# The front part of an encoder block, written as one list of operations

## The chip, the core and the metric

The kernel runs on one core of a Trainium2 chip. The metric is device time in microseconds (us) of one execution. The engines are TensorE (PE, with its weight load PEld), VectorE (DVE), ScalarE (ACT), GpSimd (POOL) and SyncE (SP), whose queue here issues all DMAs. Each engine works through its own instructions in the order in which the program has them, and waits where an operand or a buffer is not ready.

## The reference

One layer of a bidirectional encoder on 1024 tokens (a grid of 16 rows by 64 columns), with float32 inputs and output:

```python
D_MODEL, SEQ, N_HEADS, HEAD_DIM, CONV_WIDTH, D_FF = 1024, 1024, 8, 64, 512, 4096
...
u = rms_norm(x, norm1_g)
proj = u @ w_in
q, k, v, cb, cc, ch, ga, gb = split(proj)   # widths 512 x 6, 1024 x 2
q = rms_norm(q.reshape(B, S, N_HEADS, HEAD_DIM), q_norm_g)
k = rms_norm(k.reshape(B, S, N_HEADS, HEAD_DIM), k_norm_g)
y_a = neighbourhood_attention(q, k, v, rpb) @ w_attn_branch
y_b = short_gated_conv(cb, cc, ch, conv_w) @ w_conv_branch
merged = sigmoid(ga) * y_a + sigmoid(gb) * y_b
x = x + merged @ w_o
h = rms_norm(x, norm2_g) @ w_mlp_in
x = x + square(relu(h)) @ w_mlp_out

```

`rms_norm` divides by the root of the mean square plus 1e-6 and multiplies by a gain. The neighbourhood attention has 8 heads of 64, a window of 8 rows by 16 columns and a learned position bias. The convolution is depthwise with three taps.

## The kernel before

Every matrix product is made of float16 pairs: an operand is scaled by a power of two, rounded to a float16 "hi", and what is left is a float16 "lo". A product is three passes, hi x hi, hi x lo and lo x hi (`PASSES`), added in one PSUM bank. The scale of a weight follows from its largest entry or from its sum of squares, which a small matmul with a matrix of ones adds up over the 128 partitions (`all_sum`).

Tokens come in 8 blocks of 128. The first stage, up to the fourth Q unit, is the one the change rewrites. In it:

- A block of x is loaded (`load_x`), squared and summed on ACT, its reciprocal root `y` is made by small steps on DVE with a root on ACT (`rstd`), then `u` hi is a scaled copy on ACT (L453) and `u` lo the remainder on DVE (L455). `u` is turned into `UT`, with the model dimension on the partitions: blocks 0 to 2 by PE transposes (`ln_trans`, eight for hi and eight for lo), blocks 3 to 7 by a DMA transpose (`ln_turn`, L470).
- V's weights come in two halves (`cV[0]`, `cV[1]`) of two 512 KB pieces each. The hi parts are made on ACT (L313), the lo parts of the first piece on DVE (L300) and of the second on POOL (L310, L298).
- `v_unit` multiplies one block by one half of V's weights (24 matmuls of 256 columns; blocks 0 to 2) or by both (24 of 512; blocks 3 to 7).
- `sforms` makes sums and differences of quarters of the normalized x on POOL, splits them on ACT and DVE and stores them to DRAM (L522); the gate products of a later stage read them.
- Then come 8 Q units and 8 K units, each 24 matmuls of 512 columns (5.18 us from start to start). Each is followed by a chain `qk_vec`: copy and square on ACT (L610, L611), a reduction per head (L614) and `rstd` on DVE, a product (L621), hi on ACT (L628), lo on DVE (L630), and a DMA transpose of the result into `QD` or `KD` (`finish_qk`, L641). The tiles `q16` that hold hi and lo have two buffers. `QD` takes the place of x in SBUF.

Behind it stand the convolution, attention, the gates, the output projection and the MLP, all of them with PE busy nearly throughout.

What sets the order is how the Python code is run: `unit` emits a group of matmuls, and behind it a number of steps of the generators in `fg` (`step`) and of the weight preparation in `bg` (`tick`). There is no scheduler behind it; an instruction stands in its engine's queue where the code emitted it. Weight pieces go through five buffers (`rawp`), so a piece is loaded when the buffer five pieces back is free.

Of the kernel before, what the change touches and what calls it, by code (L numbers as in the profile page):

```python
# [70 lines left out]
def encoder_block(ctx: ExitStack, tc: tile.TileContext, x, weights, cols, gqk, rel, masks, out):  # L71
# [375 lines left out]
    def norm(xin, sq, u, y):  # L447

        ss = tmp()
        A.activation(sq, xin, AF.Square, accum_out=sc[:, ss])  # L450
# [2 lines left out]
        A.activation(u[:, 0], xin, AF.Copy, scale=sc[:, y])  # L453
        yield
        V.scalar_tensor_tensor(u[:, 1], xin, sc[:, y], u[:, 0], op0=OP.mult, op1=OP.subtract)  # L455

    def ln_trans(u16, b, dst):
        for s in range(2):
            pt = bank16("o")
            for k in range(8):  # L460
                T.transpose(pt[:, k * 128:(k + 1) * 128], u16[:, s, k * 128:(k + 1) * 128], ident)
            o = dst[:, s, :, b * 128:(b + 1) * 128]
            i = pt.rearrange("p (k t) -> p k t", k=8)
            if s == 0:
                A.activation(o, i, AF.Copy)
# [32 lines left out]
    SFORM = (6, 8, 10, 12)

    def sforms():  # L500

        for n, start in enumerate(SFORM):
            yield from apart(start, 0)
            assert turned[0] >= n + 5
            z = []
            for b in (n, n + 4):
                A.activation(xt[:, b], xt[:, b], AF.Copy, scale=sc[:, at(ys, b)])
# [1369 lines left out]
```

## Time and profile before

| | |
|---|---|
| time, median of 3 runs | 1233.58 us (1231.42 to 1234.42) |
| the profiled execution | 1232.41 us, its span 1230.6 us |
| PE busy | 1197.8 us, 97% |
| DVE, ACT, POOL busy | 943.2 (77%), 765.9 (62%), 432.5 us (35%) |
| mean granted clock of PE | 0.994 |
| PE busy in the first 93.7 us | 73.63 us |

A row of the page's time line gives the start (us from the span's start), the length (us), the engine, the line of the kernel, the operation, output and inputs, and, in brackets, how long the engine was idle before it and what ended that wait. "xN" means that N such instructions are taken together. A row of a stretch gives length and busy time by engine with the number of instructions, then the granted clock (1.00 is full), the share of DMA engines busy and GB/s.

### The profile page before, as it was taken

Reading aid. Unit: us, or ns where it says so; the run is one execution under the profiler, and the core shown is the slowest. Engines: PE = TensorE matmul, PEld = TensorE weight load, DVE = VectorE, ACT = ScalarE, POOL = GpSimd, SP = SyncE. Lnnn points to the kernel's source line nnn. Section 1 sums busy time; section 2 is a strip of 40 time slices with the busy share of each in tenths; the row PEclk is TensorE's granted clock in tenths of the full one; section 3 lists DMA queues with packets and bytes.
Section 4 is the critical chain, followed back from the end, with each engine's and each line's share of the span. In section 5 each row is a group of like instructions: output and inputs, shape, how many; then the busy total and the mean of one; then the engine's idle time right before and its main releaser. Section 6 shows DMA issues by size and latency. Waiting matters only on the chain.

```text
span 1230.6 us, 16688 instructions
## 1 busy us (share of the span) xinstructions
PE 1197.8 (97%) x6102; PEld 575.8 (47%) x6102; DVE 943.2 (77%) x1747; ACT 765.9 (62%) x1185; POOL 432.5 (35%) x289
## 2 busy tenths in 40 slices
PE   4989999999999999999999999999999999999998
PEld 3534445555444444444468444444444444444444
DVE  6668778898658686887878555455447899999997
ACT  6777667778645455436768687687775763646430
POOL 2340003231411111101004455665658463464562
PEclk9999999999999999999999999999999999999999
DMA  6457455567551121125197454355374924435202
GB/s 259 105 201 173 105 117 120 127 138 143 112 141 60 45 69 44 61 80 227 32 166 186 149 188 160 131 179 178 131 265 162 366 104 162 171 115 220 104 35 103
DMA packets 170867, 173.34 MB, mean 141 GB/s; under 512 B 131488, under 2 KB 132000, under 8 KB 166688
## 3 DMA queue, kind: packets, MB, share of 16 engines
q1 hardware_dynamic: 170784, 172.27, 47.0%
q8 instruction: 48, 0.79, 0.3%
q14 instruction: 35, 0.29, 0.1%
HBM read 102.51 MB, written 37.75 MB: 114 GB/s over the span
## 4 chain that ended last, share of the span: by engine, by line
PE 40%; DVE 7%; ACT 2%; issue 2%; DMA 1%; DVEq 0%; ACTq 0%
PE ps_d L207 16%; PE ps_s L207 13%; PE ps_o L207 10%; DVE ops L1710 1%; DVE w L1090 1%; DVE form L1281 1%; DVE v L1329 1%; DMA u2T<-v 1%; DMA u2x<-v 1%; DVE ops L1703 0%; DVE x L1464 0%; ACT ops L1701 0%; ACT as L1559 0%; DVE x L1808 0%; DVE as L1603 0%
## 5 line engine op out<-in xcount | busy, mean ns | idle before, releaser
L207 PEld LDWEIGHTS <-ops 128*128 128x128 f16 x1356 | 132.9, 98 | 161.0 <-issue 4.8
L207 PEld LDWEIGHTS <-w 128*128 128x128 f16 x1368 | 133.1, 98 | 143.9 <-issue 5.0
L927 PE MATMUL ps_d<-uT,w_ws 128*128 128x512 f16 x576 | 135.7, 379 | 2.0 <-DVE cv L66 2.0
L207 PE MATMUL ps_s<-ops 128*128 128x512 f16 (+1 forms) x528 | 118.4, 374 | 0.0
L207 PE MATMUL ps_d<-ops 128*128 128x512 f16 x504 | 115.6, 379 | 0.0
L207 PE MATMUL ps_d<-u2T,w 128*128 128x512 f16 (+1 forms) x504 | 110.1, 371 | 0.0
L1701 ACT ACTIVATE ops<-hf,sc 128x2048 f16<-128x2048 f32 x26 | 52.0, 1999 | 93.2 <-PE ps_d L207 51.4
L1077 POOL TENSOR_TENSOR tsum<-raw 128x512 f32<-128x512 f32 x28 | 46.5, 1676 | 148.8 <-ACT raw L959 148.8
L207 PEld LDWEIGHTS <-uT 128*128 128x128 f16 x648 | 64.6, 100 | 70.3 <-issue 6.6
L1281 POOL TENSOR_TENSOR as<-as 128x512 f32<-128x512 f32 x56 | 76.7, 1370 | 41.4 <-ACT as L1561 38.1
L207 PEld LDWEIGHTS <-w_s 128*128 128x128 f16 x588 | 56.9, 98 | 69.3 <-issue 0.9
L927 PEld LDWEIGHTS <-w_ws 128*128 128x128 f16 x576 | 55.6, 98 | 60.7 <-issue 2.6
L1703 DVE SCALAR_TENSOR_TENSOR ops<-hf,sc,ops 128x2048 f16<-128x2048 f32 x26 | 73.7, 2835 | 7.4 <-ACT ops L1701 7.4
L207 PE MATMUL ps_s<-u2x,w 128*128 128x512 f16 (+1 forms) x348 | 78.6, 375 | 0.0
L207 PE MATMUL ps_o<-ops 128*128 128x512 f16 x324 | 76.0, 385 | 2.4 <-DVE as L1604 2.4
L959 ACT ACTIVATE raw<-raw,sc 128x256 f32<-128x256 f32 x164 | 67.6, 493 | 11.1 <-DMA raw<-in_weights 11.1
L1077 POOL TENSOR_TENSOR gsum<-raw 128x512 f32<-128x512 f32 x14 | 18.7, 1353 | 128.1 <-ACT raw L959 74.4
L1094 ACT ACTIVATE w<-raw,sc 128x512 f16<-128x512 f32 (+1 forms) x28 | 24.7, 927 | 51.8 <-DVE sc L443 51.8
L1594 DVE TENSOR_TENSOR as<-ps_s,as 128x512 f32<-128x512 f32 x13 | 9.0, 691 | 57.9 <-ACT as L1613 57.9
L66 ACT ACTIVATE sz<-sz,sc 128x384 f32<-128x384 f32 (+1 forms) x64 | 37.2, 581 | 23.7 <-DVE sc L66 23.4
L207 PE MATMUL ps_o<-u2T,w 128*128 128x512 f16 (+1 forms) x204 | 45.9, 376 | 2.4 <-DVE as L1604 2.4
L207 PE MATMUL ps_d<-w_ws,uT 128*128 128x512 f16 x192 | 43.1, 379 | 1.4 <-DVE w_ws L300 1.4
(356 smaller groups left out, 2595.7 us busy)
## 6 DMA issues: line engine op xcount, KB each, us to landing
raw<-in_weights SPq DMA_DIRECT2D x89, 512.0 KB, 5.4
hs<-as SPq DMA_DIRECT2D x16, 1792.0 KB, 8.7
hf<-hs SPq DMA_DIRECT2D x26, 1024.0 KB, 5.0
w2x<-in_weights SPq DMA_DIRECT2D x16, 512.0 KB, 8.1
raw<-in_weights SPq DMA_DIRECT2D x16, 384.0 KB, 3.6
xt<-in_x SPq DMA_DIRECT2D x8, 512.0 KB, 10.0
gs<-s SPq DMA_DIRECT2D x4, 1024.0 KB, 6.2
x<-in_x SPq DMA_DIRECT2D x8, 512.0 KB, 10.2
```

Of the source, the lines that this page charges most:

```text
L66: return f(out, *a, **kw)
L207: T.matmul(ps, l, r, start=a, stop=b)
L927: T.matmul(ps, l, r, start=a, stop=b)
L959: A.activation(v, v, AF.Copy, scale=sc[:, at(g, 4 * i + k)])
L1077: G.tensor_tensor(t[:, o], a, b, op=OP.add)
L1090: V.scalar_tensor_tensor(o(1), w, sc[:, s], o(0), op0=OP.mult, op1=OP.subtract)
L1094: A.activation(o(0), w, AF.Copy, scale=sc[:, s])
L1281: sub.tensor_tensor(z[o], z[a], z[b], op=op)
L1329: V.tensor_tensor(v[:, :, 1], fv[0][:, a:b], v[:, :, 0], op=OP.subtract)
L1701: A.activation(P[:, 1, 0], hf, AF.Copy, scale=sc[:, Rs])
L1703: V.scalar_tensor_tensor(P[:, 1, 1], hf, sc[:, Rs], P[:, 1, 0], op0=OP.mult, op1=OP.subtract)
L1710: V.scalar_tensor_tensor(P[:, 0, 1, sl], w[i2], sc[:, fw], P[:, 0, 0, sl], op0=OP.mult, op1=OP.subtract)
```

## The change

The first stage is no longer the outcome of generators. A string `BEGIN` holds some 265 words, each one small operation, and a loop emits them in that order through a table `DO` from a word's name to a function. `sq.1` is the square of block 1, `ts`, `sqrt` and `y` its reciprocal root, `hi.1.P` its `u` hi on POOL, `lo.1` its `u` lo, `Th` and `Tl` its PE transposes of hi and lo, `ch` and `cl` the copies out of PSUM on the engine named, `turn.3` a DMA transpose. `tr`, `col`, `one` and `scal` find V's scales, `whi.r.i` and `wlo.r.i` make hi and lo of half a piece (with `P`: lo on POOL). `V.b.h.kind.kh` is a sixth of a V unit (4 matmuls): block, half of the weights (empty: both), pass, and half of the depth. `vh`, `vl` take V out of PSUM. `zs`, `sp`, `sh`, `sl`, `st` are the parts of `sforms`, `q...` the preparation of Q's weights, `Q.b.r` a quarter of a Q unit, `qc` to `ql` the steps of its chain, `ld...` a load of a weight piece, `ks` and `kc` the squares of K's pieces and what follows.

So PE work is cut finer and interleaved: groups of V's blocks 0 to 2 alternate, and those that need hi parts alone go ahead of those that need the weights' lo parts. `u` hi goes to POOL for all blocks but 5. x blocks are loaded earlier among the weights. The `sforms` parts run during V and the first Q units and their stores are spread. The first four Q units are in the list, their chains are partly behind it. K's scale is asked for one unit earlier. The mask's load stands behind the first transpose into `QD`. No matmul, and nothing that is computed, is added or removed.

On ACT, the first instructions before (L450 squares a block of x, L453 makes u hi, L424 is the root, L465 copies a transpose, L313 makes V's weight hi):

```order
L450 ACTIVATE sq_111,sc_71<-xt_80 128x1024
L424 ACTIVATE sc_71<-sc_71 128x1
L453 ACTIVATE u16_81<-xt_80,sc_71 128x1024
L450 ACTIVATE sq_111,sc_71<-xt_80 128x1024
L424 ACTIVATE sc_71<-sc_71 128x1
L465 ACTIVATE uT_109<-ps16_o_137 128x8x128
L313 ACTIVATE w16_v_157<-raw_87,sc_71 128x256 x4
L313 ACTIVATE w16_v_157<-raw_89,sc_71 128x256 x4
```

and now (L559 square, L567 root, L597 copy, L635 weight hi):

```order
L559 ACTIVATE sq_113,sc_71<-xt_80 128x1024
L567 ACTIVATE sc_71<-sc_71 128x1
L559 ACTIVATE sq_113,sc_71<-xt_80 128x1024 x2
L567 ACTIVATE sc_71<-sc_71 128x1
L597 ACTIVATE uT_109<-ps16_o_130 128x8x128
L635 ACTIVATE w16_v_114<-raw_87,sc_71 128x256 x4
L635 ACTIVATE w16_v_114<-raw_89,sc_71 128x256 x2
L567 ACTIVATE sc_71<-sc_71 128x1
```

The u hi rows are gone from ACT, and the squares of blocks 1 and 2 stand ahead of the copy of block 0's transpose.

On POOL, from the first weight parts on, before (`scaled` and `w16_v` are V's weight lo, `sform` the sums):

```order
L310 TENSOR_SCALAR scaled_168<-raw_89,sc_71 128x256 x4
L298 TENSOR_TENSOR w16_v_157<-scaled_168,w16_v_157 128x256 x4
L310 TENSOR_SCALAR scaled_329<-raw_94,sc_71 128x256 x4
L298 TENSOR_TENSOR w16_v_157<-scaled_329,w16_v_157 128x256 x4
L513 TENSOR_TENSOR sform_484<-xt_80 128x512 x2
```

and now (`u16` is u hi):

```order
L579 TENSOR_SCALAR u16_81<-xt_80,sc_71 128x1024 x2
L646 TENSOR_SCALAR scaled_172<-raw_87,sc_71 128x256 x2
L648 TENSOR_TENSOR w16_v_114<-scaled_172,w16_v_114 128x256 x2
L579 TENSOR_SCALAR u16_81<-xt_80,sc_71 128x1024
L646 TENSOR_SCALAR scaled_235<-raw_87,sc_71 128x256 x2
L648 TENSOR_TENSOR w16_v_114<-scaled_235,w16_v_114 128x256 x2
L646 TENSOR_SCALAR scaled_259<-raw_89,sc_71 128x256 x2
L648 TENSOR_TENSOR w16_v_114<-scaled_259,w16_v_114 128x256 x2
```

Between and ahead of the weight parts there are now the u hi of the blocks.

On ACT in the Q stage, ahead of the hi parts of K's weights (`w16_ws<-raw`, 128x512), before:

```order
L628 ACTIVATE q16_988<-qs_902 128x8x128
L610 ACTIVATE qs_991<-ps_o_917,sc_71 128x512
L611 ACTIVATE sq_992<-qs_991 128x512
L424 ACTIVATE sc_71<-sc_71 128x8
L628 ACTIVATE q16_1035<-qs_945 128x8x128
L610 ACTIVATE qs_1038<-ps_d_963,sc_71 128x512
L611 ACTIVATE sq_1039<-qs_1038 128x512
L313 ACTIVATE w16_ws_726<-raw_373,sc_71 128x512 x2
```

and now:

```order
L533 ACTIVATE q16_915<-qs_761 128x8x128
L533 ACTIVATE q16_920<-qs_808 128x8x128
L533 ACTIVATE q16_950<-qs_892 128x8x128
L515 ACTIVATE qs_952<-ps_d_864,sc_71 128x512
L516 ACTIVATE sq_953<-qs_952 128x512
L449 ACTIVATE sc_71<-sc_71 128x8
L515 ACTIVATE qs_994<-ps_o_924,sc_71 128x512
L516 ACTIVATE sq_995<-qs_994 128x512
L449 ACTIVATE sc_71<-sc_71 128x8
L336 ACTIVATE w16_ws_736<-raw_675,sc_71 128x512 x2
```

The hi parts of Q blocks 1, 2 and 3 (`q16_915`, `q16_920`, `q16_950`) now stand together, the third with the copies of units 4 and 5 and K's hi parts behind it; before, a unit's copy stood between any two of them.

The diff, cut to its core:

```diff
--- before.py
+++ after.py
+BEGIN = """
+    sq.0 ts.0 sqrt.0 tr.0 y.0 tr.1 col.0 hi.0.P lo.0 Th.0 one.0 sq.1 ts.1 sq.2 scal.0 sqrt.1 y.1 ch.0.A
...
+    gain sh.3 sl.3 vl.7. Q.2.3 qr.1 qc.2 Q.3.0 st.3 ks.2 ks.3 qh.0 vl.6. ql.0 Q.3.1 Q.3.2 Q.3.3 kc
+"""
...
-                yield from apart(units[0], 2 if self.kind in "QC" else 3)
+                yield from apart(units[0], {"Q": 2, "C": 2, "K": 1}.get(self.kind, 3))
...
     SP.dma_start(sc[:, consts], cols)
     load_upto(2)
     load_x(1)
+    load_x(2)
     load_upto(4)
-    load_x(2)
     load_x(3)
+    load_x(4)
+    load_x(5)
     load_upto(5)
+    load_x(6)
+    load_x(7)
     SP.dma_start(gq.rearrange("p a d -> p (a d)"), bass.AP(tensor=gqk.tensor, offset=gqk.offset,
                                                            ap=[[0, 128], [1, 2 * HD]]))
-    for b in range(4, 8):
-        load_x(b)
...
-    def norm(xin, sq, u, y):
-
-        ss = tmp()
-        A.activation(sq, xin, AF.Square, accum_out=sc[:, ss])
-        yield
-        yield from rstd(ss, D, y, 9)
-        A.activation(u[:, 0], xin, AF.Copy, scale=sc[:, y])
-        yield
-        V.scalar_tensor_tensor(u[:, 1], xin, sc[:, y], u[:, 0], op0=OP.mult, op1=OP.subtract)
-
...
-    SFORM = (6, 8, 10, 12)
...
-    push(cV[0])
-    ln_step(0, 2)
-    tick()
-    ln_step(0, 5)
-    ln_step(1)
-    tick(3)
-    ln_step(0)
-    ln_step(1)
-    tick(4)
-    ln_trans(u16[:, 0], 0, UT)
...
-    for p in range(11):
-        if p == 3:
-            flush()
-            push(cQ)
-        if 0 < p < 6:
-            v_unit(p % 3, p // 3, 1, 2)
-        elif p:
-            v_unit(p - 3, None, 2, 4)
-        for q in (p,) if p < 6 else (2 * p - 6, 2 * p - 5):
-            c = q // 2 + 3
-            if c < 8 and q % 2 == 0:
-                ln_step(c, 2)
-                ln_turn(u16[:, c % 4], c, UT)
-                turned[0] = c + 1
-            if c < 7:
-                ln_step(c + 1, 3)
...
+    def rows_hi(b, e):
+        o, y = u16[:, b % 4, 0], sc[:, at(ys, b)]
+        if e:
+            G.tensor_scalar(o, xt[:, b], y, 1.0, op0=OP.mult, op1=OP.mult)
+        else:
+            A.activation(o, xt[:, b], AF.Copy, scale=y)
+
+    def rows_lo(b):
+        V.scalar_tensor_tensor(u16[:, b % 4, 1], xt[:, b], sc[:, at(ys, b)], u16[:, b % 4, 0],
+                               op0=OP.mult, op1=OP.subtract)
+
+    def rows_turn(b):
+        SP.dma_start_transpose(UT[:, :, :, b * 128:(b + 1) * 128].rearrange("p s k t -> p (s k) t"),
+                               u16[:, b % 4].rearrange("p s k -> p (s k)"))
+
...
+    def v_part(r, i):
+        h, p = r // 2, r % 2
+        return [(vw[:, h, :, 256 * (4 * p + c):256 * (4 * p + c) + 256], cV[h].raw[p][:, 256 * c:256 * c + 256],
+                 sc[:, at(rv[h], 4 * p + c)]) for c in (2 * i, 2 * i + 1)]
+
+    def v_hi(r, i):
+        for w, x, s in v_part(r, i):
+            A.activation(w[:, 0], x, AF.Copy, scale=s)
+
+    def w_did(key):
+        wsum[key] = wsum.get(key, 0) + 1
+        if wsum[key] == 2:
+            done[0] += 1
+
+    def v_lo(r, i, e):
+        if e:
+            t = w1p.tile([128, 512], F32, name="scaled", bufs=2)
+            for c, (w, x, s) in enumerate(v_part(r, i)):
+                G.tensor_scalar(t[:, 256 * c:256 * c + 256], x, s, 1.0, op0=OP.mult, op1=OP.mult)
+            for c, (w, x, s) in enumerate(v_part(r, i)):
+                G.tensor_tensor(w[:, 1], t[:, 256 * c:256 * c + 256], w[:, 0], op=OP.subtract)
+        else:
+            for w, x, s in v_part(r, i):
+                V.scalar_tensor_tensor(w[:, 1], x, s, w[:, 0], op0=OP.mult, op1=OP.subtract)
+        w_did(r)
+
...
+    def v_mms(b, h, kind, kh):
+        g = vgroups.index((b, h))
+        if (kind, kh) == ("hh", 0):
+            vbank[g] = bank("ds"[g % 2])
+        ps = vbank[g][:, :512 if h is None else 256]
+        sa, sw = {"hh": (0, 0), "lh": (1, 0), "hl": (0, 1)}[kind]
+        for k in range(4 * kh, 4 * kh + 4):
+            w = vw[:, :, sw, k * 256:(k + 1) * 256] if h is None else vw[:, h, sw, k * 256:(k + 1) * 256]
+            T.matmul(ps, UT[:, sa, k, b * 128:(b + 1) * 128], w, start=(kind, k) == ("hh", 0),
+                     stop=(kind, k) == ("hl", 7))
+
+    def v_out(b, h, s):
+        ps = vbank[vgroups.index((b, h))][:, :512 if h is None else 256]
+        hi, lo = (VT[:, b, i, (h or 0) * 256:(h or 0) * 256 + (512 if h is None else 256)] for i in range(2))
+        if s == 0:
+            A.activation(hi, ps, AF.Copy, scale=2.0 ** -20)
+        else:
+            V.scalar_tensor_tensor(lo, ps, 2.0 ** -20, hi, op0=OP.mult, op1=OP.subtract)
+
...
+    def q_part(r, i, s):
+        k = 2 * r + i
+        hi, lo = (cQ.parts[:, w, 512 * k:512 * k + 512] for w in range(2))
+        x, c = cQ.raw[r][:, 512 * i:512 * i + 512], sc[:, at(wscale["q"], k)]
+        if s == 0:
+            A.activation(hi, x, AF.Copy, scale=c)
+        else:
+            V.scalar_tensor_tensor(lo, x, c, hi, op0=OP.mult, op1=OP.subtract)
+            w_did(("q", r))
+
+    def q_mms(b, r):
+        if r == 0:
+            vbank["q", b] = bank("ds"[(len(vgroups) + b) % 2])
+        for k in (2 * r, 2 * r + 1):
+            for n, (sa, sw) in enumerate(PASSES):
+                T.matmul(vbank["q", b], UT[:, sa, k, b * 128:(b + 1) * 128], cQ.parts[:, sw, 512 * k:512 * k + 512],
+                         start=(k, n) == (0, 0), stop=(k, n) == (7, 2))
+        units[0] += r == 3
+
+    qv = {}
+
+    def q_vec(b, n):
+        if b not in qv:
+            q16[b] = []
+            qv[b] = qk_vec(vbank["q", b], cQ.inv, "q", q16[b])
+        for _ in range(n):
+            advance(qv[b])
+
...
+    for word in BEGIN.split():
+        name, *args = word.split(".")
+        DO[name](*[None if name in ("V", "vh", "vl") and a == "" else int(a) if a.isdigit() else a for a in args])
+
+    for b in range(4):
+        q_vec(b, 0)
+        fg.append(qv[b])
+
     for n, (kind, b) in enumerate(todo):
         ch = cQ if kind == "q" else cK
-        if b == 0:
-            push(cK if kind == "q" else cConv[0])
-        ps = bank("do"[n % 2])
-        q16[n] = []
-
-        def post(ps=ps, kind=kind, n=n, ch=ch):
-            fg.append(qk_vec(ps, ch.inv, kind, q16[n]))
-        unit(tok_mms(ps, actU, b, ch, 8, 512, 0), post, 4, 3)
-        if n == 3:
-            forced[0] = True
-            while formed[0] < 4:
-                step()
-            forced[0] = False
+        if kind == "k" and b == 0:
+            push(cConv[0])
+        if n == 4:
             QD = base.tile([128, 4, 2, 2, S], F16, name="qD", tag="Q")
             KD = base.tile([128, 8, S], F16, name="kD", tag="K")
             pln.close()
@@ -663,12 +774,19 @@
             pbias = ExitStack()
             wbias = pbias.enter_context(tc.tile_pool(name="pbias", bufs=2))
             mk = wbias.tile([128, 2, 384], BF16, name="mk", bufs=1)
-            SP.dma_start(mk, masks)
             cneg, cinv = keep(), keep()
             V.tensor_scalar(sc[:, cneg], sc[:, isgq], -(2.0 ** -15), None, op0=OP.mult)
             V.tensor_scalar(sc[:, cinv], sc[:, sgq], 2.0 ** 15, None, op0=OP.mult)
+            finish_qk(0)
+            SP.dma_start(mk, masks)
             bias = {0: bias_load(0)}
-        if n >= 3:
+        if n >= 4:
+            ps = bank("do"[n % 2])
+            q16[n] = []
+
+            def post(ps=ps, kind=kind, n=n, ch=ch):
+                fg.append(qk_vec(ps, ch.inv, kind, q16[n]))
+            unit(tok_mms(ps, actU, b, ch, 8, 512, 0), post, 4, 4 if n < 8 else 3)
             finish_qk(n - 3)
         if n in (5, 6):
             bias_make(*bias[0], n - 5)
```

More of the change, by code (lines that the diff above doesn't have):

```diff
@@ new lines, in rows_hi, with rows_trans @@
+    def rows_hi(b, e):
[7 more added lines that the diff above has]
+                               op0=OP.mult, op1=OP.subtract)
+    pt = {}
+    def rows_trans(b, s):
+        pt[b, s] = bank16("o")
+        for k in range(8):
+            T.transpose(pt[b, s][:, k * 128:(k + 1) * 128], u16[:, b % 4, s, k * 128:(k + 1) * 128], ident)
```

183 lines of the change are left out of this document (110 added, 73 removed).

## The prediction

> **What bounds the kernel now.** I read the page, then the busy time by stretches of the span, then TensorE (PE) in order of time. In the stretches the columns are length, busy PE, PEld, DVE, ACT, POOL, granted clock, DMA share, GB/s.
>
> ```profile
> 0.00:93.70 93.70, 73.63 (x411) 40.98 (x412) 63.26 (x136) 68.16 (x109) 32.94 (x37) 0.96 0.59 189
> 93.70:166.30 72.60, 72.60 (x340) 32.91 (x339) 58.30 (x173) 47.54 (x89) 1.83 (x2) 1.00 0.64 137
> ...
> 24.00:26.00 2.00, 1.76 (x17) 1.49 (x15) 1.55 (x8) 0.36 (x2) 0.29 (x1) 0.50 0.00 0
> ```
>
> From 93.7 us PE is never idle until attention; before it PE idles 20.1 us and part of its work runs at clock 0.50. The kernel is PE work in a fixed order, so this front part is where time can be had.
>
> ```profile
> 9.63 0.16 PE L198 MATMUL ps_o<-ones 128*128 128x1 bf16 x1 [9.63 <-DVE ones L342]
> ...
> 13.18 4.50 PE L207 MATMUL ps_d<-w_v,uT 128*128 128x256 f16 x23 [0.34 <-DVE w_v L300]
> 18.14 0.62 PE L461 MATMUL ps_o<-ident,u 128*128 128x128 f16 x8 [0.47 <-ACT u L453]
> ...
> 23.62 0.18 PE L198 MATMUL ps_o<-ones 128*128 128x1 bf16 x1 [3.54 <-DVE ones L342]
> ...
> 38.41 2.78 PE L207 MATMUL ps_d<-w_v,uT 128*128 128x256 f16 x24
> 41.03 5.34 PE L207 MATMUL ps_s<-w_v,uT 128*128 128x512 f16 x24
> 46.21 5.34 PE L207 MATMUL ps_d<-w_v,uT 128*128 128x512 f16 x24
> ...
> 64.31 7.04 PE L207 MATMUL ps_s<-w_v,uT 128*128 128x512 f16 x24 [2.37 <-DMA uT<-u]
> ...
> 93.71 5.34 PE L207 MATMUL ps_d<-w_ws,uT 128*128 128x512 f16 x24
> ...
> 114.46 5.34 PE L207 MATMUL ps_d<-w_ws,uT 128*128 128x512 f16 x24
> 119.64 5.34 PE L207 MATMUL ps_o<-w_ws,uT 128*128 128x512 f16 x24
> ```
>
> From start to start a V group of half width takes 2.62 us (38.41 to 41.03), one of full width 5.18 (41.03 to 46.21), eight transposes 0.62. After a gap of 3.54 us the clock row shows 0.50, and after one of 2.37 us a group takes 7.04 instead of 5.34. The fifth Q unit starts at 93.71, the first K unit (K0) at 114.46, the second (K1) at 119.64. From the fifth Q unit on, PE's order is the same in both kernels; on the other engines it is the same soon behind. So I work out how much earlier K1 starts. A shift there moves all that follows.
>
> **PE's own work.** Six half V groups, five whole ones, four Q units and six sets of transposes: 6 x 2.62 + 9 x 5.18 + 6 x 0.62 = 66.0 us. Before takes 93.7 for it: 20.1 idle, the other 7.6 mostly at half clock. The change removes none of this work, it only closes gaps.
>
> **Start of V.** The list puts the squares of blocks 1 and 2 on ACT ahead of the copy of block 0's transpose, and x2 is now loaded ahead of V's second pair of pieces.
>
> ```profile
> 5.81 0.20 ACT L424 ACTIVATE sc<-sc 128x1 f32<-128x1 f32 x1 [0.22 <-DVE sc L423]
> 6.95 0.15 DVE L426 RECIPROCAL sc<-sc 128x1 f32<-128x1 f32 x1
> ...
> 7.52 0.16 DVE L432 SCALAR_TENSOR_TENSOR sc<-sc 128x1 f32<-128x1 f32 x1
> ...
> 9.12 1.06 ACT L450 ACTIVATE sq<-xt 128x1024 f32<-128x1024 f32 x1 [0.25 <-DMA xt<-in_x]
> 10.08 0.18 ACT L450 ACTIVATION_READ_ACCUMULATOR sq<-xt 128x1 f32 x1
> ...
> 11.02 1.01 ACT L465 ACTIVATE uT<-ps_o 128x1024 f16<-128x1024 f16 x1
> ...
> 11.92 3.29 ACT L313 ACTIVATE w_v<-raw,sc 128x256 f16<-128x256 f32 x8
> ```
>
> ```profile
> 10.00:20.00 10.00, 7.71 (x55) 5.33 (x52) 8.17 (x19) 7.25 (x17) 5.00 (x8) 1.00 0.98 388
> ```
>
> x1 lands at 9.1; x2, 0.52 MB behind it at 388 GB/s, at 10.45. Its square ends 1.14 later (9.12 to 10.26 in the row), 11.6; a root 0.2, the copy 1.0: 12.8; three weight pieces at 3.29/8 = 0.41: 14.05. V starts there, 1.6 later than the 12.47 of its first matmul before. Two of six transpose sets are done: 14.05 + 66.0 - 1.2 = 78.85 for the fifth Q unit, if PE then never waits and is at full clock. The first stretch is at half clock: 23 matmuls took 4.50 where full clock gives 23 x 0.109 = 2.5; **+2.0** (0 to 4: none, or the same loss on twice as many matmuls): 80.85.
>
> **POOL against DVE.** Seven of eight u-hi scalings move from ACT to POOL, and four of the eight half-piece lo parts of V's weights stay there but are spread out. DVE makes the lo parts of u beside them.
>
> ```profile
> L760 POOL TENSOR_SCALAR cv<-cv,sc 128x1024 f32<-128x1024 f32 x4 | 4.5, 1122 | 53.8 <-DVE sc L66 42.7 <-ACT P L66 11.1
> ...
> L298 POOL TENSOR_TENSOR w_v<-scaled,w_v 128x256 f16<-128x256 f32 x8 | 5.3, 692 | 5.6 <-ACT w_v L313 5.6
> ...
> L310 POOL TENSOR_SCALAR scaled<-raw,sc 128x256 f32<-128x256 f32 x8 | 4.1, 535 | 19.5 <-DVE sc L273 10.7 <-issue 8.8
> ```
>
> ```profile
> L300 DVE SCALAR_TENSOR_TENSOR w_v<-raw,sc,w_v 128x256 f16<-128x256 f32 x8 | 4.1, 574 | 0.0
> ```
>
> ```profile
> 43.13 1.28 DVE L455 SCALAR_TENSOR_TENSOR u<-xt,sc,u 128x1024 f16<-128x1024 f32 x1 [2.77 <-ACT u L453]
> ...
> 47.14 2.50 POOL L513 TENSOR_TENSOR sform<-xt 128x512 f32<-128x512 f32 x2 [11.62 <-ACT xt L507]
> ...
> 48.40 2.32 DVE L455 SCALAR_TENSOR_TENSOR u<-xt,sc,u 128x1024 f16<-128x1024 f32 x1 [0.61 <-ACT u L453]
> ...
> 49.72 2.13 POOL L513 TENSOR_TENSOR sform<-sform,xt 128x512 f32<-128x512 f32 x1
> ```
>
> The same DVE instruction takes 1.28 alone and 2.32 beside POOL, whose own goes from 1.25 to 2.13: they took turns. From 12.65, when block 1's scale is ready (its square and root end at 11.8, then the four DVE steps that took 6.95 to 7.68 for block 0), POOL has four scalings and four weight halves, 4 x 1.12 + 4 x 2 x (0.535 + 0.692) = 14.3; DVE has four u-lo parts and two weight halves, 5.1 + 4 x 0.574 = 7.4. In turns this ends at 34.4; in parallel POOL ends at 27. PE reaches V.0.1.hl.0, which needs the last of it, after thirty quarter groups of 0.437 and four transpose sets: 14.05 + 13.1 + 2.5 + 2.0 = 31.65. So PE waits 0 to 2.75. I take **+2.5**, near the upper end, as the long rows add up almost whole: 83.35. Behind it the list has room: V.3 needs a DMA transpose issued near 29, and V.4 to V.7 theirs five us apart.
> [...]
>
> **K's weights.** In front of K0 stand the per-unit chains of four Q blocks, which the list has pushed together.
>
> ```profile
> 106.80 0.22 DVE L273 TENSOR_SCALAR sc<-sc 128x8 f32<-128x8 f32 x1
> ...
> 116.35 1.40 DVE L300 SCALAR_TENSOR_TENSOR w_ws<-raw,sc,w_ws 128x512 f16<-128x512 f32 x2
> 117.68 1.22 DVE L630 TENSOR_TENSOR q<-qs,q 128x1024 f16<-128x1024 f32 x1
> ```
>
> ```profile
> 109.48 0.69 ACT L610 ACTIVATE qs<-ps_d,sc 128x512 f32<-128x512 f32 x1 [0.70 <-PE ps_d L207]
> 110.20 0.63 ACT L611 ACTIVATE sq<-qs 128x512 f32<-128x512 f32 x1
> 110.73 2.54 ACT L313 ACTIVATE w_ws<-raw,sc 128x512 f16<-128x512 f32 x4
> ...
> 115.73 1.04 ACT L628 ACTIVATE q<-qs 128x1024 f16<-128x1024 f32 x1
> ```
>
> ```profile
> 119.20 0.69 DVE L621 TENSOR_TENSOR qs<-qs,sc 128x512 f32<-128x512 f32 x1
> 119.81 0.68 DVE L614 TENSOR_REDUCE sc<-sq 128x8 f32<-128x512 f32 x1
> ```
>
> ```profile
> DMA to landing us min/median/max: 4.3/5.4/6.0
> ```
>
> (The last is of the qD transposes.) Units and blocks are counted from 0. Let t be the start of Q unit 2, 83.35 - 10.36 = 73.0. ACT takes unit 2's copy and square at t + 5.4 (0.69 + 0.63), then two K squares (about 1.2 each, as those of x), then q hi of block 0 (1.04): t + 10.1; DVE's q lo (1.22): t + 11.3. Two reductions and three products (0.61 each from start to start, 119.20 to 119.81), that block's own q lo of 1.2 and some twenty small steps, with ACT's roots, unit 3's copy and block 1's q hi in between, end block 1's q lo at about t + 18.2. The q tiles have two buffers, so q hi of block 3 waits for block 1's transpose: + 5.4 = t + 23.6. On ACT everything stands behind it: q hi to 24.65, copies and squares of units 4 and 5 with a root, 28.45; the reduction and K's scale at t + 29.2. Before, that scale stood 7.7 us ahead of K0; now K0 is due at t + 31.1, 1.9 ahead. Eight K lo parts (0.70 each) with a q product, bias, q lo and a reduction among them (about 3) end at t + 38.3, K1 can start at t + 38.8 instead of t + 36.3: **+2.5**. Bounds: 0, if the transpose lands in 4.3 and DVE is quicker; 5, if the parts take the 10.95 of before (106.80 to 117.75) and the transpose 6.0.
>
> **Edits at nothing.** The sum and difference forms (POOL, ACT, DVE) go from V and the first Q unit into V and the Q units: POOL has 32.9 of 93.7 us busy, and their four stores are read in attention. Loads of Q and K pass SP behind transposes whose inputs are older. The mask's load goes behind the first qD transpose, about 2 us of SP, and its reader is a bias step 17 us later. Q's weights: scale 1 us after V.5, sixteen parts while V.6 and V.7 (10.4 us) run.
>
> **Sum.** K1 at 73.0 + 38.8 = 111.8 instead of 119.64: 7.8 us less. The profiled execution took 1232.41 (span 1230.6), so 1224.6; it lay 1.2 below the median 1233.58, so I say **1225**.
>
> **Rivals.** (1) No turn-taking and no wait at K0: 2.5 + 2.5 more, 1220. For it: DVE's idle time in the new Q stage; against: the rows of 2.32 and 2.13. (2) The gain is eaten: one more transpose round ahead of K's scale, 5.4 + 1.04 + 1.22 = 7.7, leaves 1232.5. For it: the two buffers; against: PE's wait itself lets DVE and ACT catch up. (3) Slower: two such rounds, q hi of blocks 3 and 4 each behind a transpose with ACT's K pieces behind them. K0 then starts 15 us late, 1240. It decides once K's scale comes later than t + 40.8, 11.6 after my sum; the transposes' rows (at most 6.0) speak against it.
>
> **Chances.** Forecast 0.60, (1) 0.22, (2) 0.07, (3) 0.11. A measurement tells 0.3%, 3.7 us: faster 0.82, same 0.07, slower 0.11. The range, 1218.5 to 1230.5, takes in (1) and the upper bounds of the POOL and K terms (0.25 + 2.5 more) with some 2 us for waits I don't see; out of it are (2) and (3).
>
> **What would show it.** V's first matmul near 14 and no PE gap above 2.3 us behind it; clock 0.50 once at most; u lo parts on DVE above 1.28 and a PE wait for w_v at 32 to 35; the fifth Q unit near 83; q hi of block 3 idle for a qD transpose; PE waiting in K0 for w_ws, K1 near 112; from there each row earlier by the same amount. Wrong would be: a fifth Q unit after 88, K0 waiting over 8 us, or PE gaps in attention that before didn't have.

## The result and the profile after

| | before | after |
|---|---|---|
| time, median of five runs each | 1233.58 us (1231.42 to 1234.42) | 1227.87 us (1225.94 to 1228.82) |
| span of the profiled execution | 1230.6 us | 1226.3 us |

The ratio is 0.9953, 95% interval 0.9939 to 0.9968: faster by 5.7 us. Forecast was 1225, with a range of 1218.5 to 1230.5.

First the stretches of the kernel after: up to its fifth Q unit, the same length of time behind that as was shown of before, and two microseconds inside K0. The columns are length, busy PE, PEld, DVE, ACT and POOL, granted clock, DMA share, GB/s.

```profile
0.00:84.99 84.99, 69.89 (x412) 40.22 (x413) 65.91 (x130) 58.70 (x99) 47.79 (x44) 1.00 0.65 205
84.99:157.60 72.61, 69.95 (x316) 31.05 (x315) 56.32 (x168) 46.17 (x88) 2.36 (x2) 0.98 0.64 135
...
112.00:114.00 2.00, 1.99 (x5) 0.69 (x5) 2.00 (x5) 0.21 (x1) 0.00 (x0) 0.50 0.75 209
```

The front part took 93.7 us and takes 85.0; PE idles 15.1 us in it instead of 20.1, and the granted clock reads 1.00 over it. (Matmuls run at half rate at its beginning even so: those of 256 columns follow each other at 0.213 us there and later at 0.109; the last section has the times.) What follows had no idle PE before; now PE waits there 2.7 us and runs at half clock for a while (0.50 in the last row above). So 8.7 us are won and 5.1 of them lost again right behind. PE in order of time shows where:

```profile
14.54 1.20 PE L665 MATMUL ps_d<-w_v,uT 128*128 128x256 f16 x4 [1.80 <-ACT w_v L635]
...
35.32 0.67 PE L665 MATMUL ps_s<-w_v,uT 128*128 128x256 f16 x3
37.11 0.27 PE L665 MATMUL ps_s<-w_v,uT 128*128 128x256 f16 x1 [1.13 <-DVE w_v L651]
...
62.35 0.38 PE L708 MATMUL ps_s<-w_ws,uT 128*128 128x512 f16 x1
63.43 2.10 PE L708 MATMUL ps_s<-w_ws,uT 128*128 128x512 f16 x9 [0.71 <-DVE w_ws L700]
66.43 3.18 PE L708 MATMUL ps_s<-w_ws,uT 128*128 128x512 f16 x14 [0.89 <-DVE w_ws L700]
...
84.99 5.34 PE L230 MATMUL ps_d<-w_ws,uT 128*128 128x512 f16 x24
...
105.73 0.38 PE L230 MATMUL ps_d<-w_ws,uT 128*128 128x512 f16 x1
106.29 1.47 PE L230 MATMUL ps_d<-w_ws,uT 128*128 128x512 f16 x6 [0.18 <-DVE w_ws L323]
108.22 0.81 PE L230 MATMUL ps_d<-w_ws,uT 128*128 128x512 f16 x3 [0.46 <-DVE w_ws L323]
109.54 0.97 PE L230 MATMUL ps_d<-w_ws,uT 128*128 128x512 f16 x3 [0.51 <-DVE w_ws L323]
112.01 4.20 PE L230 MATMUL ps_d<-w_ws,uT 128*128 128x512 f16 x11 [1.50 <-DVE w_ws L323]
116.05 5.34 PE L230 MATMUL ps_o<-w_ws,uT 128*128 128x512 f16 x24
```

There are three places. From 35.32 to 37.22 four matmuls of 256 columns take 1.90 us and are worth 4 x 0.109 = 0.44, 1.5 lost. Q unit 0 starts at 62.35, unit 1 at 69.45: 7.10 instead of 5.18, 1.9 lost. K0 starts at 105.73 and K1 at 116.05: 10.32 instead of 5.18, 5.1 lost. Of these 5.1, 1.5 are clock: the last eleven matmuls take 4.20, and in five runs below, behind the same wait of 1.50, 2.73. The fifth Q unit comes 8.72 earlier than before, K1 only 3.59. The end comes another 0.8 earlier: a wait of PE for `ones` of 0.69 us, at 993 us before, is gone, and the other waits behind K1 differ by a few tenths both ways.

Who makes PE wait, on DVE, POOL and ACT in order of time:

```profile
32.28 4.78 DVE L651 SCALAR_TENSOR_TENSOR w_v<-raw,sc,w_v 128x256 f16<-128x256 f32 x4
32.52 2.85 POOL L729 TENSOR_TENSOR sform<-xt 128x512 f32<-128x512 f32 x2
...
55.40 2.29 DVE L736 TENSOR_TENSOR s<-sform,s 128x2048 f16<-128x2048 f32 x1 [1.95 <-ACT s L733]
57.60 8.77 DVE L700 SCALAR_TENSOR_TENSOR w_ws<-raw,sc,w_ws 128x512 f16<-128x512 f32 x7
57.77 3.39 POOL L729 TENSOR_TENSOR sform<-xt 128x512 f32<-128x512 f32 x2 [4.35 <-DVE s L736]
...
67.50 0.74 DVE L700 SCALAR_TENSOR_TENSOR w_ws<-raw,sc,w_ws 128x512 f16<-128x512 f32 x1
...
98.89 1.06 ACT L533 ACTIVATE q<-qs 128x1024 f16<-128x1024 f32 x1 [5.13 <-DMA qD<-q]
...
104.22 0.22 DVE L296 TENSOR_SCALAR sc<-sc 128x8 f32<-128x8 f32 x1
...
112.70 1.40 DVE L323 SCALAR_TENSOR_TENSOR w_ws<-raw,sc,w_ws 128x512 f16<-128x512 f32 x2
```

Twice DVE's lo parts lie beside a sum form on POOL: four of V's take 4.78 us, seven of Q's 8.77. The means hide that only some of them were held up. Single instructions, one of DVE and one of POOL from each place:

```profile
32.52 1.45 POOL L729 TENSOR_TENSOR sform<-xt 128x512 f32<-128x512 f32 x1
32.76 1.49 DVE L651 SCALAR_TENSOR_TENSOR w_v<-raw,sc,w_v 128x256 f16<-128x256 f32 x1
...
57.77 1.72 POOL L729 TENSOR_TENSOR sform<-xt 128x512 f32<-128x512 f32 x1 [4.35 <-DVE s L736]
58.27 1.76 DVE L700 SCALAR_TENSOR_TENSOR w_ws<-raw,sc,w_ws 128x512 f16<-128x512 f32 x1
```

Three of V's four parts take 1.48 or 1.49 us, and four of Q's seven take 1.75 or 1.76; Q's other three, begun before POOL's operations or after them, take 0.74 or 0.75. In K0 it is the chain of the prediction: q hi of block 3 waits 5.13 us for the transpose of an earlier block, K's scale (104.22) stands behind it, and the last lo parts end at 114.1.

### The profile page after: what moved, and what is told of

Its sections match the earlier page's. It is cut to its first block, busy times and chain, and to the rows that moved or that the text cites. A ratio compares the mean times of both kernels' runs of the same rounds, so it can differ in the third digit from the quotient of the medians.

```text
span 1226.3 us, 16695 instructions
## 1 busy us (share of the span) xinstructions
PE 1196.1 (98%) x6102; PEld 575.4 (47%) x6102; DVE 945.6 (77%) x1747; ACT 757.3 (62%) x1178; POOL 447.7 (37%) x296
## 4 chain that ended last, share of the span: by engine, by line
PE 62%; DVE 7%; ACT 2%; issue 2%; DMA 1%; DVEq 0%; ACTq 0%
PE ps_d L230 24%; PE ps_s L230 22%; PE ps_o L230 16%; DVE w L1208 1%; DVE ops L1828 1%; DMA raw<-in_weights 1%; DMA u2T<-v 1%; DVE w_s L1208 1%; PE ps_d L1045 0%; DVE sg L1331 0%; ACT as L1677 0%; DVE ops L1821 0%; ACT w_s L1212 0%; DVE m L1333 0%; DVE as L1721 0%
## 5 line engine op out<-in xcount | busy, mean ns | idle before, releaser
L230 PEld LDWEIGHTS <-uT 128*128 128x128 f16 x288 | 28.4, 99 | 38.5 <-issue 6.3
L1793 POOL TENSOR_TENSOR t<-raw,w2x 128x1024 f32<-128x1024 f32 x6 | 21.4, 3565 | 66.0 <-DMA w2x<-in_weights 41.0
```

What stands on the lines that cost most here:

```text
L230: T.matmul(ps, l, r, start=a, stop=b)
L1793: G.tensor_tensor(T2[:, i], w12[i], w22[i], op=OP.add)
```

## The experiments

Theory: PE runs through the front part, slowed by POOL and DVE taking turns, and the gain is cut in K0 because the q tiles have two buffers. Rivals: DVE and ACT are simply full there, whatever the buffers; or something else paces V. Each experiment changes the kernel after. Times are medians; a ratio is to the kernel before, run beside it, with its 95% interval.

**Buffers for q.** The tiles of Q blocks 2 and 3 are laid into the two buffers of the split sum forms, which are free by then.

```diff
-        t = wqk.tile([128, 8, 2, r, HD], F16, name=kind + "16", tag="q16")
+        n, q16n[0] = q16n[0], q16n[0] + 1
+        if n in (2, 3):
+            t = wqk.tile([128, 4, 2, 512], F16, name="q16s", tag="s16", bufs=2)[:, :2].rearrange(
...
+        else:
+            t = wqk.tile([128, 8, 2, r, HD], F16, name=kind + "16", tag="q16")
```

> Edit: the q tiles of blocks 2 and 3 lie in the buffers of the sum forms (free by then), so that q hi of block 3 no longer waits for the qD transpose of block 1. All else as in the changed kernel. Theory (the transpose round sets K's scale): q hi of block 3 comes near 93 instead of 98.9, K's scale near 99.5 instead of 104.2, before K0 is due at 105.7; the last K lo part ends near 109, PE waits under 1 us in K0 instead of 5.1, K1 starts at 111 to 112 instead of 116.05, and the time is about 1223.5 (4 to 5 us under the changed kernel). Rival (the backlog on DVE and ACT sets it: the five units' chains and the K parts take that long anyway, and the 5.1 us of ACT's idle time are only shifted): K's scale moves by under 1.5 us, K1 starts after 114.5, the time stays within 1.5 us of 1227.9.

1223.18 us, ratio 0.9924 (0.991 to 0.9939). q hi of block 3 on ACT, K's scale on DVE and K0 with K1 on PE:

```profile
94.58 1.06 ACT L538 ACTIVATE q16s<-qs 128x1024 f16<-128x1024 f32 x1 [0.94 <-DVE qs L526]
...
99.92 0.22 DVE L296 TENSOR_SCALAR sc<-sc 128x8 f32<-128x8 f32 x1
...
105.60 5.34 PE L230 MATMUL ps_d<-w_ws,uT 128*128 128x512 f16 x24
110.78 5.34 PE L230 MATMUL ps_o<-w_ws,uT 128*128 128x512 f16 x24
```

The scale comes 4.3 us earlier, PE has no wait in K0, K1 comes 5.3 earlier. The theory holds; the backlog of DVE and ACT does not set it. The whole loss in K0, clock included, hung on the buffer.

**Q chains earlier.** The other way to the same end: the first two blocks' chains are written out earlier in the list.

```diff
-    gain sh.3 sl.3 vl.7. Q.2.3 qr.1 qc.2 Q.3.0 st.3 ks.2 ks.3 qh.0 vl.6. ql.0 Q.3.1 Q.3.2 Q.3.3 kc
+    qh.0 gain ql.0 sh.3 qr.1 qq.1 qy.1 sl.3 vl.7. Q.2.3 qc.2 Q.3.0 st.3 qh.1 ks.2 ks.3 ql.1 vl.6. Q.3.1 Q.3.2 Q.3.3 kc
```

> Edit: in the list alone, the chains of Q blocks 0 and 1 (root, product, q hi, q lo) are written out ahead of the last sum form's split and K's last two squares; two buffers as in the changed kernel. Theory (the wait is for block 1's transpose, wherever its time comes from): q hi of block 0 comes near 78 instead of 85.3, q hi of block 1 near 84 instead of 91.8, block 1's transpose lands near 91, q hi of block 3 waits no longer, K's scale comes near 99.5, K1 starts at 111 to 112.5 instead of 116.05, time about 1223.5 to 1224.5. Rival (ACT and DVE are full there; what is put first delays K's squares and the forms as much): K's squares and with them K's sum come 3 us or more later, K1 stays within 1.5 us of 116, time within 1.5 us of 1227.9.

1223.81 us, ratio 0.9933 (0.9918 to 0.9948); the two q hi came at 77.30 and 82.27, K's scale at 100.4. One short wait is left in K0:

```profile
105.15 3.11 PE L230 MATMUL ps_d<-w_ws,uT 128*128 128x512 f16 x13
108.79 2.73 PE L230 MATMUL ps_d<-w_ws,uT 128*128 128x512 f16 x11 [0.53 <-DVE w_ws L323]
111.36 5.34 PE L230 MATMUL ps_o<-w_ws,uT 128*128 128x512 f16 x24
```

Both ends of the same wait lead to the same K1, within 0.6 us.

**Forms later.** Sum form 2, and the split of form 1 ahead of it, go behind Q's lo parts.

```diff
-    V.6..hh.0 sh.1 qscal V.6..hh.1 V.6..lh.0 sl.1 st.0 sp.2 qhi.0.1 ...
+    V.6..hh.0 sh.1 qscal V.6..hh.1 V.6..lh.0 st.0 qhi.0.1 ...
...
-    qlo.1.1 ldK.1 ldK.0 V.7..hl.1 Q.0.0 sh.2 vl.4. ... qlo.3.1 Q.0.3 ...
+    qlo.1.1 qlo.3.1 sl.1 st.1 sp.2 ldK.1 ldK.0 V.7..hl.1 Q.0.0 vl.4. ... Q.0.3 ...
...
-    Q.1.2 zs.3 ks.0 sl.2 ks.1 sp.3 vl.5. st.2 Q.1.3 vh.7. ldK.2 qc.0 qr.0 qc.1 ... gain sh.3 sl.3 vl.7. ...
+    Q.1.2 zs.3 ks.0 ks.1 vl.5. Q.1.3 vh.7. ldK.2 qc.0 sh.2 qr.0 sl.2 sp.3 st.2 qc.1 ... ql.0 sh.3 sl.3 st.3 Q.3.1 ...
```

> Edit: in the list alone, sum form 2 (POOL) and the split of form 1 on DVE go behind the last lo part of Q's weights, and the splits of forms 2 and 3 behind that. Theory (turn-taking of POOL and DVE doubles Q's lo parts): these parts take 0.75 us each instead of 1.25, the last ends near 63 instead of 68.2, PE no longer waits in Q0 and the stretch from Q0's first matmul to Q1's is 5.2 instead of 7.1; the fifth Q unit starts near 83.1 instead of 84.99. What K1 does then tells a second thing: if the chain hangs on unit 2's start, K1 moves by the same 1.9 to about 114.1 and the time to 1226; if the forms, now beside the q chains, delay those, K1 stays at 116 or comes later and the time stays at 1228 or above. Rival (Q's lo parts are slow for another reason, such as waiting for the hi parts on ACT): each still takes over 1 us, and the fifth Q unit stays at 84.5 or later.

1237.9 us, ratio 1.0043 (1.0028 to 1.0059): slower than before. PE and ACT in order of time:

```profile
61.79 5.34 PE L708 MATMUL ps_s<-w_ws,uT 128*128 128x512 f16 x24
66.97 5.34 PE L708 MATMUL ps_d<-w_ws,uT 128*128 128x512 f16 x24
...
71.12 1.06 ACT L284 ACTIVATE w_ws<-raw 128x1024 bf16<-128x1024 f32 x1 [7.86 <-DMA raw<-in_weights]
...
82.51 5.34 PE L230 MATMUL ps_d<-w_ws,uT 128*128 128x512 f16 x24
97.02 0.16 PE L221 MATMUL ps_s<-ones 128*128 128x1 bf16 x1 [9.17 <-DVE ones L289]
```

The first half of the theory holds: Q0 takes 5.18, and the fifth Q unit starts at 82.51, 2.5 earlier. (The edit moves form 2 and the split of form 1 at once; which of the two counts for how much stays open.) But the store `st.1` waits on SP for the late split, and K's loads stand behind it on that queue: ACT stands 7.9 us in front of K's first square, and the copy of Q unit 0 behind it. K's last square then comes at 90.48, the sum's reduction on DVE stands behind form 3's split (94.41 to 96.7), and the sum, which stands on PE ahead of unit 5, holds PE for 9.2 us. The loss came about two queues away from the edit.

**K's sum late.** The one edit of the change in the weight preparation undone.

```diff
-                yield from apart(units[0], {"Q": 2, "C": 2, "K": 1}.get(self.kind, 3))
+                yield from apart(units[0], {"Q": 2, "C": 2}.get(self.kind, 3))
```

> Edit: K's column sum waits for three units of distance again instead of one (the one part of the change in the split of weights undone); all else as in the changed kernel. Theory (the scale's place on DVE counts, since K0 now has no spare time): the sum's matmul and with it K's scale come about two units, 10 us, later than 104.2, K0 waits 12 to 15 us in all, K1 starts near 126, time 1237 to 1239, slower than before. Rival (the scale is bound by q hi of block 3 in any case): K's scale stays within 2 us of 104.2 and the time within 2 us of 1227.9.

1232.41 us, ratio 1.0003 (0.9991 to 1.0016): the gain is gone. The sum's matmul came at 99.98 instead of 90.17, as the theory has it, but K's scale only 5.7 us later (109.95) and K1 at 119.93, not 126: the scale had been held by q hi anyway, so the first four microseconds of the delay cost nothing. Both theory and rival were half right.

**x2's square later.** V's first matmul waited for a hi part of its weights on ACT, behind the square of block 2.

```diff
-    ... sq.1 ts.1 sq.2 scal.0 sqrt.1 y.1 ch.0.A hi.1.P whi.0.1 whi.0.0 Tl.0 ts.2 ...
+    ... sq.1 ts.1 scal.0 sqrt.1 y.1 ch.0.A hi.1.P whi.0.0 whi.0.1 sq.2 Tl.0 ts.2 ...
```

> Edit: in the list alone, the square of block 2 goes from ahead of the copy of block 0's transpose to behind the first four hi parts of V's weights, and these stand in the order in which PE reads them. Theory (PE runs through V once it has begun, so that a later start of V costs its whole size): V's first matmul comes at 13.2 to 13.8 instead of 14.54, the fifth Q unit about 1 us earlier than 84.99, K1 about 115, time 1226.5 to 1227. Rival (V is paced by u and the weights' parts, not by its start): block 2's u comes 1 us later, PE waits for it inside V, the fifth Q unit stays at 84.7 or later, time as the changed kernel's 1227.9 within 1.

1226.63 us, ratio 0.9952 (0.9937 to 0.9968), no difference to the kernel after. PE in order of time:

```profile
12.29 1.57 PE L665 MATMUL ps_d<-w_v,uT 128*128 128x256 f16 x4 [0.46 <-ACT w_v L635]
...
57.44 5.35 PE L665 MATMUL ps_d<-w_v,uT 128*128 128x512 f16 x24
...
85.27 5.34 PE L230 MATMUL ps_d<-w_ws,uT 128*128 128x512 f16 x24
...
112.20 2.73 PE L230 MATMUL ps_d<-w_ws,uT 128*128 128x512 f16 x11 [1.50 <-DVE w_ws L323]
```

V starts 2.25 us earlier and the fifth Q unit 0.3 later: the theory falls. PE lost the time again inside V, in waits (0.21 us at 14.9, 0.54 at 21.8, 0.20 at 32.4) and at half rate, which lasted 1.2 us longer (6.6 us behind V's first matmul instead of 5.4). V's start alone does not set its end. (The last row is K0's, at full clock behind the same wait; this is where the 1.3 us at K1, 114.77, come from.)

**u hi on ACT.** The seven scalings that the change gave to POOL, given back.

```diff
-    sq.0 ts.0 sqrt.0 tr.0 y.0 tr.1 col.0 hi.0.P lo.0 ...
+    sq.0 ts.0 sqrt.0 tr.0 y.0 tr.1 col.0 hi.0. lo.0 ...
```

> Edit: the seven u hi scalings that the change gives to POOL go back to ACT, at the same places of the list. Theory (turn-taking costs a little, but ACT has no room in V: it is busy nearly throughout from 9.9 to 30 us): seven times about 1.1 us more on ACT make PE wait in V, the fifth Q unit comes at 87 to 91 instead of 84.99, and the time is 1229 to 1233. Rival (the turns of POOL and DVE cost more than ACT's load): u lo parts take 1.28 us throughout, the fifth Q unit comes at 83.5 or earlier, and the time is 1226.5 or less.

1232.53 us, ratio 1.0003 (0.9993 to 1.0014). V starts at 16.02 behind 3.30 us of idle PE, V.6 waits 2.24 us and runs at half clock (7.03 us for 5.34), the fifth Q unit comes at 92.04, seven later, K1 at 122.41. The move relieves ACT, which is worth more than the turns it brings, and without it nothing of the gain is left. The change's other parts in V, the finer interleaving and the earlier loads of x, were not undone one by one; what each is worth is not shown.

**All later forms.** The buffers, the early chains and the later forms together, with K's loads ahead of `st.1`.

> Edit: three things together. Q tiles of blocks 2 and 3 in the form buffers, as in the run on the buffers; form 2 and the split of form 1 behind Q's lo parts, as in the run on the forms, but with K's loads issued ahead of the store that waits for that split; chains of Q blocks 0 and 1 written out in the list ahead of form 3's split. Theory (the wait in Q0 and that in K0 are separate causes, each to be had on its own): no wait in Q0 (1.9 to 2.4 us), fifth Q unit at 82.5 to 83.1, no wait in K0 (5.1), K1 at 108.4 to 109, time 1220 to 1221. Rival (the forms moved out of Q0's way must be made somewhere, and there they hold up the q chains or K's squares): PE waits over 2 us in units 5, 6 or K0, K1 at 111 or later, time 1223 or more.

1225.0 us, ratio 0.9936 (0.9923 to 0.9949). Q0 has no wait and the fifth Q unit starts at 83.13, but the rival's wait is there:

```profile
87.13 1.04 ACT L284 ACTIVATE w_ws<-raw 128x1024 bf16<-128x1024 f32 x1
...
90.46 0.16 PE L221 MATMUL ps_s<-ones 128*128 128x1 bf16 x1 [1.99 <-DVE ones L289]
90.49 7.03 PE L230 MATMUL ps_o<-w_ws,uT 128*128 128x512 f16 x24
```

K's last square stands behind form 3's split on ACT; PE waits 2 us for the sum and pays 1.7 more at half clock (7.03 for 5.34). K0 has waits of 1.80 and 0.53 too, and K1 starts at 115.75.

**Both starts.** The same with the later square of x2.

> Edit: the edits of the run with later forms and that of the later square of block 2 together. Theory: the two add up; the fifth Q unit 1 us earlier than in the run with later forms alone, K1 about 107.5 to 108, time 1219 to 1220. Rival (something behind V's start paces V): as the run with later forms, within 0.5 us at K1.

1225.73 us, ratio 0.9944 (0.993 to 0.9958): the rival. V starts at 12.46 instead of 14.67, and the fifth Q unit at 83.95, not earlier than the 83.13 of the run above. This agrees with the run on x2's square, but is weaker than it looks: PE stayed at half rate 3.6 us longer than in the run above (9.1 us behind V's first matmul instead of 5.4), which takes up to 1.8 us of the earlier start.

**Forms mended.** In that list K's last two squares go right behind the copy of Q unit 1, and block 2's reduction ahead of form 3's split.

```diff
-    ... qc.1 qr.1 qq.1 gain ... qy.1 qh.1 ks.2 ql.1 qc.2 sh.3 sl.3 ks.3 st.3 Q.3.0 vl.6. Q.3.1 ...
+    ... qc.1 ks.2 ks.3 qr.1 qq.1 gain ... qy.1 qh.1 ql.1 qc.2 qr.2 vl.6. sh.3 sl.3 st.3 Q.3.0 Q.3.1 ...
```

> Edit: the list of the run with all later forms, with two things mended: K's last two squares stand on ACT right behind the copy of Q unit 1, ahead of form 3's split, and the reduction of Q block 2 stands ahead of that split on DVE. Theory (in that run unit 5 waited because K's column sum stands in front of it on PE and its last square stood behind form 3's split, 87.1 us): that square ends before 80, PE has no wait ahead of unit 5, K's scale comes near 100, no or under 1 us of wait in K0; Q0 without wait as there; fifth Q unit near 83.1, K1 at 109 to 110, time 1221 to 1222. Rival (DVE and ACT are simply full between 66 and 105 once the forms lie there): PE still waits over 2 us in units 5, 6 or K0, K1 at 111 or later, time 1223 or more.

1224.4 us, ratio 0.9932 (0.9918 to 0.9945). The wait ahead of unit 5 shrinks to 0.36, but K0 loses 3.3 again. SP's queue and DVE:

```profile
88.23 4.71 SPq L551 DMA_TRANSPOSE qD<-q  x1
93.03 0.53 SPq L786 DMA_DIRECT2D mk<-in_masks  x1
93.61 0.49 SPq L503 DMA_DIRECT2D bias<-in_rel  x1
...
98.48 0.62 DVE L509 SCALAR_TENSOR_TENSOR bias<-bias,sc,mk 128x384 f32<-128x384 f32 x1 [3.40 <-DMA bias<-in_rel]
...
101.74 0.21 DVE L296 TENSOR_SCALAR sc<-sc 128x8 f32<-128x8 f32 x1
```

The bias load stands on SP behind form 3's store and the first qD transpose, DVE's bias step waits for it, and K's scale stands behind that step. (The wait was there in the run with all later forms, 3.20 us, and not in the kernel after.)

**u lo of block 4 later.** In V, form 0 is moved away from DVE's lo parts.

```diff
-    ... V.2.1.hh.0 hi.4.P zs.0 wlo.2.1.P lo.4 V.1.1.hh.1 ... zs.4 ... wlo.3.1. sq.6 ts.7 ...
+    ... V.2.1.hh.0 wlo.2.1.P hi.4.P zs.0 V.1.1.hh.1 ... wlo.3.1. lo.4 sq.6 zs.4 ts.7 ...
```

> Edit: the list of the mended run, and in V: u lo of block 4, the scaling of x4 and with it sum form 0 go behind V's last lo part on DVE, u hi of block 4 behind V's last lo part on POOL, and the copy of form 1 on ACT goes behind Q's hi parts. Theory (the wait of 33 to 37 us is the turn-taking of form 0 on POOL with V's lo parts on DVE): these parts take 0.42 to 0.75 us each instead of 1.2 and end 2 to 4 us earlier, PE's stretch from 33.15 to 37.2 shrinks by 1.5 to 2.3, V.7 and the fifth Q unit come 1.5 to 2.3 earlier than in the mended run, near 81.2, K1 near 107.5, time 1219.5 to 1220.5. Rival (then u of blocks 5 to 7 comes late, since sum form 0 now stands in front of their u hi on POOL): the wait moves to V.6 or V.7, the fifth Q unit stays within 0.7 us of the mended run's.

1223.61 us, ratio 0.9928 (0.9915 to 0.994). DVE, then PE:

```profile
31.19 1.66 DVE L656 SCALAR_TENSOR_TENSOR w_v<-raw,sc,w_v 128x256 f16<-128x256 f32 x4
```

```profile
33.91 1.90 PE L670 MATMUL ps_d<-w_v,uT 128*128 128x512 f16 x8 [0.90 <-DMA uT<-u]
...
52.19 5.35 PE L670 MATMUL ps_s<-w_v,uT 128*128 128x512 f16 x24 [0.81 <-DMA uT<-u]
```

The same four lo parts take 1.66 us instead of 4.78, which shows the turn-taking by itself. At most the 1.5 us that PE loses there could be won. But PE now waits 0.90 and 0.81 us for the transposes of u, V.7 starts at 57.45 against 56.48 in the mended run and the fifth Q unit at 83.36 against 82.39: the wait moved, as the rival had it, by even more than it allowed. The two times do not differ.

**Bias first.** The mended run, with the loads of mask and bias ahead of the first qD transpose and form 3's store behind it.

```diff
-            finish_qk(0)
             SP.dma_start(mk, masks)
             bias = {0: bias_load(0)}
+            finish_qk(0)
+            DO["st"](3)
```

> Edit: the mended run, and on the DMA queue of SP the loads of the mask and of the first bias go ahead of the first qD transpose, and the store of sum form 3 behind it. Theory (in the mended run DVE stood 2.8 us in front of the first bias step, whose load was issued at 93.6 behind a store that waited for form 3's split and behind that transpose, and K's scale stood behind the bias step): the bias step has no wait, K's scale comes at 98.5 to 99.5 instead of 101.7, PE waits under 1 us in K0 instead of 3.3, K1 at 109 to 110 instead of 112.1, time 1221 to 1222.5. Rival (the scale is bound by the q chains of blocks 2 and 3 all the same, or block 3's q hi now waits for the later store): K's scale after 101, K1 at 111.5 or later, time 1223.5 or more.

1221.89 us, ratio 0.9921 (0.9906 to 0.9936), the lowest median of all, though its interval overlaps with that of the buffers alone.

```profile
98.30 0.22 DVE L296 TENSOR_SCALAR sc<-sc 128x8 f32<-128x8 f32 x1
...
103.63 5.34 PE L230 MATMUL ps_d<-w_ws,uT 128*128 128x512 f16 x24
108.81 5.34 PE L230 MATMUL ps_o<-w_ws,uT 128*128 128x512 f16 x24
```

From Q0 to K1 PE waits 0.33 us in all, ahead of unit 5; K1 starts 7.2 us earlier than in the kernel after, 10.8 earlier than before.

## Why the prediction was right, and where it was off

Faster was right, and by the mechanism named: a gain in front, cut in K0. The time was missed by 2.9 us; K1 came at 116.05 instead of 111.8. Of these 4.3 us, 1.6 lie ahead of the fifth Q unit (84.99, forecast 83.35) and 2.6 in K0 (5.1 lost, forecast 2.5).

- **Start of V and PE's own work.** V's first matmul came at 14.54 (forecast 14.05), Q0 at 62.35 (forecast 83.35 - 4 x 5.18 = 62.63). That Q0 fits so closely is partly luck, as the terms ahead of it missed in both directions: V's start by +0.5, the half clock by +0.6, POOL by -1.0, and the transposes, which the sum takes at the 0.62 of their rows where they follow each other at 0.45, by -0.7; small waits add 0.3. And "if PE then never waits" was the wrong model: V's start can move by 2.25 us without moving its end.
- **Half clock, +2.0.** From 14.54 to 19.80 PE works at half its rate: 16 matmuls and two sets of transposes take 5.26 us and are worth 16 x 0.109 + 2 x 0.45 = 2.6, so 2.6 are lost.
- **POOL against DVE, +2.5.** The loss is 1.5, from 35.3 to 37.2 (forecast: a wait at 32 to 35). The mechanism, turns of POOL and DVE, was right, the partners were not: I reckoned with u hi beside u lo, and the wait came from V's lo parts beside sum form 0, which stood under "edits at nothing"; in the run with u lo of block 4 later they are short again. u lo itself took 1.28 to 1.49 us up to 30 us; the longer rows (2.14 and 2.29) came later. That the size is near is luck.
- **Q's weights, at nothing.** This step failed. "Sixteen parts while V.6 and V.7 run" counted their number and not their neighbours: form 1's split (2.29 us) stands on DVE ahead of the lo parts, and form 2 on POOL makes four of these eight 1.75 us long instead of 0.74. Cost 1.9 us; the runs with later forms take it away. The sum and difference forms, put at nothing because POOL had room, cost DVE time in both places.
- **K's weights, +2.5.** The chain held step by step: q hi of block 3 at t + 24.3 (forecast t + 23.6), K's scale at t + 29.6 (t + 29.2), the last lo part at t + 39.5 (t + 38.3), with t = 74.63. One of its steps held by luck: the two copies, two squares and the root between t + 24.65 and t + 28.45 add up to 2.84 us, not 3.8, and the rest came as a wait of ACT for DVE of 0.96, which the sum does not name. The loss was 5.1, just above the upper bound of 5. This term is mis-sized: 1.2 us in the chain up to the last lo part, and 1.5 for the clock that fell to 0.50 behind the last wait, which I had in the list of signs and not in the sum. The second share need not come: five other profiled executions with that wait don't have it (2.73 instead of 4.20). That the buffer causes the loss, the first two runs show from both sides.
- **Loads at nothing.** Right for the kernel after. It held only while K's scale was late for another reason: in the mended run the bias's load, behind form 3's store, the first transpose and the mask's load, cost 3.4 us on DVE.
- **Rivals.** Of the first, no wait in K0 and no turn-taking, the buffers alone bring the half that lies in K0 (1223.18), and the last run, with the wait in V still there (1.13 us), comes near its 1220. The second and third did not come about: one round of transposes was waited for, not two or three. The one kernel that was clearly slower, that with later forms, was so by a queue.

## What to carry to other kernels

Work that was put "beside" a busy engine had a price there: DVE's lo parts, 0.47 and 0.74 us alone, took 1.48 and 1.75 beside POOL's sums. So look for the partner of every moved operation, not only for a free engine. When this stage was closed up, among the next waits were one for a buffer (q's, 5.13 us of ACT) and one for a load (the bias's, 3.40 us of DVE) that so far had slack; so list the slack of each buffer and load before counting the gain. And a wait that is removed shows only what it hid: taking away V's late start or the slow lo parts, one at a time, moved nothing. No run takes away both.
